# A second bank for the products with v of the later query blocks, and a later weight-norm sum, in a hybrid attention and mLSTM block

## The chip, the core and the metric

The kernel is one program on one core of a Trainium2 chip. The metric is device time in microseconds of a whole execution: 1434.75 us before the change, the median of three runs (1434.04, 1434.75 and 1437.02).

## What is computed

One layer of a streaming encoder block over a sequence of 1024 positions and 1024 channels. Inputs are normalised and multiplied with one wide projection; its columns feed a differential-attention branch with 8 heads and an mLSTM branch with 8 heads. Both are gated, projected, merged, projected once more and added to the input, and a last norm follows. The change touches the attention branch and the preparation of weights. For one head and one block of 128 queries the reference computes

```
logits = einsum("pbhqd,pbhkd->pbhqk", qb, k) + bias          # p: the two halves of the head
probs  = softmax(where(mask, logits, NEG_INF), axis=-1)
attn   = probs[0] - lam * probs[1]
out    = einsum("bhqk,bhkv->bhqv", attn, v)
```

and then normalises `out` over its 128 columns, scales it and multiplies it by SiLU of a gate.

## The kernel before

All large products are done in float16 with the operands split into a high and a low half, so that one product takes three matmuls (high by high, high by low, low by high). TensorE streams one long list of such projections, in "units" of 256 weight columns. A unit is either plain (96 matmuls of 512 columns, lines 329 to 331) or by rows (192 matmuls of 256 columns, lines 358 to 360). A unit takes 32 steps of the main loop. Beside the unit that runs, the loop issues in each step a piece of the next unit's preparation and pieces of one "side": the attention of a head or the mLSTM of a head. An attention head h runs beside the two units (q and k, then v and gate) of head h+1, that is 288 matmuls, 64 steps. The last head, 7, runs beside four gate units.

**Preparation of a unit** (`prep`). ScalarE squares and sums the two halves of the weights (line 245), VectorE adds the two sums (line 159), a matmul with ones adds them over the partitions (line 165), VectorE makes a power of two out of it (lines 135 to 139), and then ScalarE and VectorE write the high and the low half of the weights in four pieces each (lines 257 and 259). Between the squares and the sum there are two empty steps.

**Attention of a head** (`attention`). There are eight query blocks i = 0 to 7; block i has (i+1) x 128 keys. Its pieces are:
- `q` i: the first scores (line 812, into the two-bank tile psb), VectorE adds the bias and takes the extremum (line 822), ScalarE takes the exponential (line 826).
- `r` i: the second scores in the same way, then the combination of the two (line 837), and its split into a high and a low half (ScalarE line 844, VectorE line 845), which one DMA transposes (line 847, in SyncE's queue).
- `v` i: the product with v, 3 x (i+1) matmuls of 128 columns (lines 855 to 857) into a quarter of a bank, and ScalarE's sum of squares of it (line 858). Four blocks share one bank.
- `f` half: GpSimd makes the norm factors of four blocks (lines 862 to 864). `o` half: VectorE scales the four quarters of the bank by them and by the gate (line 870). `t` half: the result is split and transposed (lines 547 to 549).

**What sets the order.** `PLAN_A` gives for each piece the step of the unit loop at which it is issued (the number times 8/7), for heads 0 to 6; `PLAN_C` does it for head 7, and is not changed. A scheduler then orders the issued instructions of each engine anew: an instruction issued earlier has the higher claim, but one whose operands or whose tile are not free by its own reckoning is passed by others. On the chip each engine then works through its list in order, and waits where a semaphore is not yet set.

**PSUM.** There are eight banks: three for the projections (pp), two as one tile for scores (psb), two for small products (pmi: transposes, norm sums, and in the mLSTM the state updates) and one for the products with v (pvp). Since pvp is one bank, block 4 of a head can begin only when VectorE has scaled blocks 0 to 3 out of it (line 870). Matmuls also wait for ScalarE's read of the bank they write: block 5 waits for the squares of block 4.

Of the kernel before, what the change touches and what calls it, by code (L numbers as in the profile page):

```python
# [32 lines left out]
OFF_GATE = (9232, 10256)  # L33
BIG = 3.0e38
RING = 15
PLAN_A = [(0, 'q0'), (0, 'r0'), (0, 'q1'), (3, 'r1'), (4, 'q2'), (5, 'r2'), (9, 'q3'), (9, 'r3'), (9, 'q4'), (10, 'v0'), (14, 'v1'), (16, 'r4'), (17, 'q5'), (18, 'v2'), (19, 'r5'), (21, 'q6'), (24, 'r6'), (25, 'q7'), (27, 'r7'), (28, 'v3'), (29, 'v4'), (29, 'v5'), (30, 'f0'), (30, 'o0'), (31, 'v6'), (31, 'v7'), (42, 't0'), (55, 'f1'), (55, 'o1'), (55, 't1')]
PLAN_C = [(0, 'q0'), (0, 'r0'), (6, 'q1'), (7, 'r1'), (7, 'q2'), (9, 'r2'), (16, 'q3'), (19, 'r3'), (19, 'q4'), (19, 'r4'), (19, 'v0'), (22, 'v1'), (22, 'v2'), (25, 'q5'), (28, 'r5'), (29, 'q6'), (31, 'v3'), (32, 'v4'), (33, 'r6'), (37, 'q7'), (38, 'f0'), (38, 'r7'), (46, 'o0'), (52, 'v5'), (52, 'v6'), (63, 'v7'), (64, 'f1'), (67, 'o1'), (82, 't1'), (83, 't0')]
PLAN_M = [(0, '00gate'), (0, '01k0'), (2, '02k1'), (4, '03s0'), (5, '04s1'), (8, '05e0'), (9, '06p0'), (11, '07e1'), (13, '08p1'), (14, '09c0'), (19, '10g00'), (19, '11g01'), (20, '12g02'), (21, '13cp0'), (22, '14bs0'), (22, '15g10'), (25, '16g11'), (25, '17g12'), (26, '18cp1'), (30, '19bs1'), (30, '20g20'), (30, '21g21'), (31, '22cp2'), (32, '23bs2'), (33, '24ch'), (37, '25n0'), (47, '26t0'), (50, '27n1'), (55, '28t1')]
PLAN_N = [(0, '00gate'), (1, '01k0'), (1, '02k1'), (8, '03s0'), (10, '04s1'), (13, '05e0'), (13, '06p0'), (15, '07e1'), (16, '08p1'), (22, '09c0'), (25, '10g00'), (26, '11g01'), (26, '12g02'), (26, '13cp0'), (30, '14bs0'), (31, '15g10'), (36, '16g11'), (37, '17g12'), (40, '18cp1'), (42, '19bs1'), (43, '20g20'), (44, '21g21'), (53, '22cp2'), (54, '23bs2'), (59, '24ch'), (61, '25n0'), (67, '26t0'), (70, '27n1'), (71, '28t1')]
# [9 lines left out]
def block_kernel(ctx, tc, x, norm_w, w_in, lam, subln_w, rel_bias, conv_w, conv_b, b_if,  # L49
# [18 lines left out]
    def nm(p):  # L68
        uid[0] += 1
        return f"{p}{uid[0]}"  # L70
# [5 lines left out]
    def R(dt=F32, shape=None, p="r"):  # L76
        return ring.tile(shape or [P, S], dt, tag="t4", name=nm(p))
# [7 lines left out]
    def sm(cols=1, dt=F32, p="s", bufs=6):  # L85
        return small.tile([P, cols], dt, tag=f"{p}{cols}", name=nm(p), bufs=bufs)
# [7 lines left out]
    def m_ps():  # L94
        return pmi.tile([P, 512], F32, tag="pmi", name=nm("pmi"))

    def v_ps():
        return pvp.tile([P, 512], F32, tag="pvp", name=nm("pvp"))

    def junk(w):  # L100
        return wpool.tile([P, S], BF, tag="junk", name=nm("junk"), bufs=1)[:, :w]
# [129 lines left out]
    def wparts(shape):  # L231
        return wpool.tile([P, 2] + shape, F16, tag="wp", name=nm("wp"), bufs=WP)

    def prep(w, rowscale=None, keep=False):
        wd = w.width
        if rowscale is not None:
            g.tensor_tensor(w.wt[0], w.wt[0], rowscale[:, 0:4].unsqueeze(2).to_broadcast([P, 4, wd]), op=ALU.mult)
            yield
            for k in range(4, 8):
                s.activation(w.wt[k // 4][:, k % 4, :], w.wt[k // 4][:, k % 4, :], AF.Copy, scale=rowscale[:, k:k + 1])  # L240
            yield
        ss = sm(cols=2, p="wss")
        for k in range(2):
            j = junk(4 * wd).rearrange("p (a b) -> p a b", a=4)
            s.activation(j, w.wt[k], AF.Square, accum_out=ss[:, k:k + 1])  # L245
            yield
        yield
        yield
        w.sb = sm(p="sb")
        w.isb = sm(p="isb", bufs=8)  # L250
        fnorm_finish(ss, w.sb, w.isb)
        yield
        w.parts = {}

        def split(name, src, dst):
            w.parts[name] = dst
            s.activation(dst[0], src, AF.Copy, scale=w.sb)  # L257
            yield
            v.scalar_tensor_tensor(dst[1], src, w.sb, dst[0], op0=ALU.mult, op1=ALU.subtract)  # L259
            yield  # L260

        if keep:
            t = [R(F16, [P, KC, 256], p="wo") for _ in range(2)]
        for k in range(0, KC, 2):
            src = w.wt[k // 4][:, k % 4:k % 4 + 2, :]
            if keep:
                dst = (t[0][:, k:k + 2, :], t[1][:, k:k + 2, :])
            else:
                u = wparts([2, 256])
                dst = (u[:, 0, :, :wd], u[:, 1, :, :wd])  # L270
            yield from split(k // 2, src, dst)
# [25 lines left out]
    class Unit:  # L297
# [13 lines left out]
        def start_prep(self):  # L311
            if self.prepping is None:
                self.finish_load()
                self.prepping = prep(self.w, self.rowscale and self.rowscale(), self.keep)
                self.left = 16

        def prep_step(self):
# [479 lines left out]
    def attention(h, plan):  # L797
        (Q, K, negc, strip), (vr, gz, eps) = live.pop(("qk", h)), live.pop(("vz", h))
        bb = BB
        v.tensor_copy(bb[:, 768:1024], strip)  # L800
        rr = sm(cols=16, p="rr", bufs=2)
        rc = sm(cols=16, p="rc", bufs=2)
        ssq = sm(cols=8, p="ssq", bufs=2)
        E, AT, ops, zs = {}, {}, {}, {}

        def qk(i, p):
            n = (i + 1) * P
            sp = s_ps()
            for c in range(0, n, 512):
                e = min(n, c + 512)  # L810
                for j in range(2):
                    te.matmul(sp[:, c:e], Q[:, p, i * P:(i + 1) * P], K[p][:, j, c:e],  # L812
                              start=(j == 0), stop=(j == 1))
            if i >= 4 or p == 0:
                z = R(p="z")
            else:
                z = zs.pop(i)
            if i < 4 and p == 0:
                zs[i] = z[:, 512:]
                z = z[:, :512]  # L820
            mx = sm(p="mx")
            v.tensor_tensor_reduce(z[:, :n], sp[:, :n], bb[:, S - n:], negc, BIG, op0=ALU.add,  # L822
                                   op1=ALU.min, accum_out=mx)
            if p == 0:
                v.tensor_scalar(mx, mx, lnc, None, op0=ALU.add)  # L825
            s.activation(z[:, :n], z[:, :n], AF.Exp, bias=mx, scale=-1.0,  # L826
                         accum_out=rr[:, 2 * i + p:2 * i + p + 1])
            E[i, p] = z

        def combine(i):  # L830
            n = (i + 1) * P
            v.reciprocal(rc[:, 2 * i:2 * i + 2], rr[:, 2 * i:2 * i + 2])
            nb = sm(p="nbeta")
            v.scalar_tensor_tensor(nb, rr[:, 2 * i:2 * i + 1], nlam, rc[:, 2 * i + 1:2 * i + 2],
                                   op0=ALU.mult, op1=ALU.mult)
            A = E[i, 0]
            v.scalar_tensor_tensor(A[:, :n], E[i, 1][:, :n], nb, A[:, :n], op0=ALU.mult, op1=ALU.add)

        def turn(i):

            n = (i + 1) * P
            A = E.pop((i, 0))
            hl = E.pop((i, 1)).bitcast(F16)
            s.activation(hl[:, :n], A[:, :n], AF.Copy)
            v.tensor_tensor(hl[:, n:2 * n], A[:, :n], hl[:, :n], op=ALU.subtract)
            AT[i] = b3(A.bitcast(F16))
            nc.sync.dma_start(AT[i][:, :2 * (i + 1), :], hl[:, :2 * n], transpose=True)

        def pv(i):
            if i % 4 == 0:  # L850
                ops[i // 4] = v_ps()
            o = ops[i // 4][:, i % 4 * P:(i % 4 + 1) * P]
            at = AT.pop(i)
            for j in range(i + 1):
                te.matmul(o, at[:, j, :], vr[:, 0, j, :], start=(j == 0), stop=False)  # L855
                te.matmul(o, at[:, j, :], vr[:, 1, j, :], start=False, stop=False)
                te.matmul(o, at[:, i + 1 + j, :], vr[:, 0, j, :], start=False, stop=(j == i))
            s.activation(junk(P), o, AF.Square, scale=rc[:, 2 * i:2 * i + 1], accum_out=ssq[:, i:i + 1])

        def factor_of(qh):  # L860
            f = fac[qh] = sm(cols=4, p="fac", bufs=2)
            g.tensor_scalar(f, ssq[:, qh * 4:qh * 4 + 4], 1.0 / P, eps, op0=ALU.mult, op1=ALU.add)
            g.tensor_tensor(f, f, mhalf[:, 0:4], op=ALU.pow)
            g.tensor_tensor(f, f, rc.rearrange("p (i two) -> p i two", two=2)[:, qh * 4:qh * 4 + 4, 0], op=ALU.mult)

        def scaled_of(qh):
            on[qh] = half_tile("on")
            for j in range(4):
                i = qh * 4 + j
                v.scalar_tensor_tensor(on[qh][:, j * P:(j + 1) * P], ops[qh][:, j * P:(j + 1) * P],  # L870
                                       fac[qh][:, j:j + 1], gz[:, i], op0=ALU.mult, op1=ALU.mult)

        def rows_of(qh):
            finish_y(h, qh, on[qh], -17)

        def both(i):
            qk(i, 1)
            combine(i)
            turn(i)

        fac, on = {}, {}
        pieces = dict(q=lambda i: qk(i, 0), r=both, v=pv, f=factor_of, o=scaled_of, t=rows_of)
        for _, name in plan:
            pieces[name[0]](int(name[1:]))
            yield
# [140 lines left out]
    for h in range(H - 1):  # L1026
        phases.append((da_units(h + 1), lambda h=h: attention(h, PLAN_A), PLAN_A))
    phases.append((ga, lambda: attention(H - 1, PLAN_C), PLAN_C))
# [7 lines left out]
    first = order[0]  # L1036
# [107 lines left out]
    for ch in range(4):  # L1144
        w, so = wo[ch].w, [None, None]
# [76 lines left out]
```

## Time and profile before

| | before |
|---|---|
| runs | 1434.04, 1434.75, 1437.02 us; median 1434.75 |
| profiled execution | 1435.78 us, of which the span of the instructions is 1433.9 us |
| granted TensorE clock, mean | 0.995 |
| VectorE, ScalarE, GpSimd busy | 848.0 us (59%), 735.0 us (51%), 157.5 us (11%) |
| stage of heads 0 to 7, about | 90 to 580 us |

The profile is of one execution. Matmuls are pipelined: one of 256 columns is shown as 0.27 us long, but they follow each other at 0.11 us. An "idle" time of TensorE in the rows is therefore what remains when the one before has been shown to its end, and is some 0.16 us less than what was lost. In the timeline rows the columns are: start in us from the span's start, duration, engine, line, operation, output and inputs, form, count, and in brackets the idle time before it with what ended it.

### The profile page before, as it was taken

The numbers are of one execution on the slowest core, as the hardware profiler recorded it, in microseconds if no ns is written. First come the engines' busy times: TensorE is split into PE (matmuls) and PEld (weight loads), VectorE is DVE, ScalarE is ACT, GpSimd is POOL, SyncE is SP. The second block draws the span as 40 slices with busy tenths as digits, with TensorE's granted clock in tenths as the row PEclk, the third lists the DMA queues.
The fourth block names the chain that finished last, engine by engine and source line by source line (L and its number), as shares of the span: only waits on it lengthen the run. The fifth ranks groups of instructions, "written<-read, shape, count | busy, mean of one in ns | idle before, by whom it ended". The sixth has DMA issues, their size and how long they took to land.

```text
span 1433.9 us, 25050 instructions
## 1 busy us (share of the span) xinstructions
PE 1380.6 (96%) x9650; PEld 913.3 (64%) x9650; DVE 848.0 (59%) x2310; ACT 735.0 (51%) x1533; POOL 157.5 (11%) x215
## 2 busy tenths in 40 slices
PE   6989999999999999999999999999999999999997
PEld 3656575665756655444486787778769675444786
DVE  6276868677686756533445674775866564233633
ACT  7276556565566667832353444443435344644542
POOL 2001010010100100100102020220211200122004
PEclk9999999999999999999999999999999999999999
DMA  6456355463554645543321313231232135534303
GB/s 200 68 142 140 83 107 124 104 141 82 114 121 91 136 95 130 163 149 125 96 74 60 104 31 101 47 87 47 66 97 75 60 86 158 168 103 162 118 16 118
DMA packets 232585, 150.14 MB, mean 105 GB/s; under 512 B 117297, under 2 KB 209730, under 8 KB 232466
## 3 DMA queue, kind: packets, MB, share of 16 engines
q1 hardware_dynamic: 218450, 123.28, 35.0%
q10 hardware_dynamic: 14016, 25.27, 5.3%
q8 instruction: 75, 1.23, 0.3%
q14 instruction: 44, 0.36, 0.1%
HBM read 90.12 MB, written 18.55 MB: 76 GB/s over the span
## 4 chain that ended last, share of the span: by engine, by line
PE 77%; DVE 9%; ACT 4%; DMA 4%; POOL 3%; issue 3%; SPq 0%; POOLq 0%; DVEq 0%; ACTq 0%
PE pp L329 14%; PE pp L331 14%; PE pp L330 14%; PE pp L360 8%; PE pp L358 8%; PE pp L359 8%; PE psb L812 3%; DVE z L822 3%; DMA z<-z 2%; ACT z L826 1%; DMA qw<-rows_d 1%; DVE wp L259 1%; PE psb L908 1%; PE pvp L855 1%; DVE hl L600 1%
## 5 line engine op out<-in xcount | busy, mean ns | idle before, releaser
L358 PE MATMUL pp<-wp,X 128*128 128x256 f16 x1280 | 349.7, 273 | 0.0
L359 PE MATMUL pp<-wp,X 128*128 128x256 f16 x1280 | 349.7, 273 | 0.0
L360 PE MATMUL pp<-wp,X 128*128 128x256 f16 x1280 | 349.7, 273 | 0.0
L329 PE MATMUL pp<-X,wp 128*128 128x512 f16 x768 | 291.7, 380 | 0.3 <-ACT wp L257 0.3
L331 PE MATMUL pp<-X,wp 128*128 128x512 f16 x768 | 291.3, 379 | 0.6 <-DVE wp L259 0.6
L330 PE MATMUL pp<-X,wp 128*128 128x512 f16 x768 | 291.8, 380 | 0.0
L257 ACT ACTIVATE wp<-wt,sb 128x512 f16<-128x512 f32 x208 | 136.9, 711 | 105.4 <-DVE sb L138 70.6
L331 PEld LDWEIGHTS <-wp 128*128 128x128 f16 x1024 | 100.0, 98 | 119.7 <-DVE wp L259 1.2
L245 ACT ACTIVATE junk<-wt 128x1024 bf16<-128x1024 f32 x112 | 118.1, 1055 | 100.0 <-DMA wt<-in_w_in_dram 89.7
L329 PEld LDWEIGHTS <-wp 128*128 128x128 f16 x1024 | 100.2, 98 | 103.0 <-issue 1.7
L330 PEld LDWEIGHTS <-wp 128*128 128x128 f16 x1024 | 100.1, 98 | 97.1
L259 DVE SCALAR_TENSOR_TENSOR wp<-wt,sb,wp 128x512 f16<-128x512 f32 x208 | 150.5, 760 | 14.4 <-ACT wp L257 12.8
L359 PEld LDWEIGHTS <-X 128*128 128x128 f16 x1280 | 125.3, 98 | 18.4 <-issue 2.4
L358 PEld LDWEIGHTS <-X 128*128 128x128 f16 x1280 | 125.4, 98 | 16.8 <-issue 0.8
L360 PEld LDWEIGHTS <-X 128*128 128x128 f16 x1280 | 125.3, 98 | 14.6
L826 ACT ACTIVATE z<-z,mx 128x256 f32<-128x256 f32 (+7 forms) x128 | 99.0, 773 | 61.7 <-DVE mx L825 46.1
L822 DVE CUSTOM_DVE_ANT_0 z<-psb,BB,negc 128x256 f32<-128x256 f32 (+7 forms) x128 | 104.1, 813 | 19.7 <-PE psb L812 19.4
L331 PE MATMUL pp<-Y,wp 128*128 128x512 f16 x256 | 97.1, 379 | 0.0
L330 PE MATMUL pp<-Y,wp 128*128 128x512 f16 x256 | 97.1, 379 | 0.0
L329 PE MATMUL pp<-Y,wp 128*128 128x512 f16 x256 | 97.1, 379 | 0.0
L649 DVE SCALAR_TENSOR_TENSOR acc<-up,wcol,acc 128x512 f32<-128x512 f32 x96 | 78.0, 827 | 27.4 <-POOL acc L650 24.5
L812 PE MATMUL psb<-K,Q 128*128 128x512 f16 (+3 forms) x384 | 83.5, 326 | 7.8 <-DMA K<-hl 4.6
(245 smaller groups left out, 2012.1 us busy)
## 6 DMA issues: line engine op xcount, KB each, us to landing
wt<-in_w_in_dram SPq DMA_DIRECT2D x128, 256.0 KB, 3.4
wt<-in_w_in_dram SPq DMA_DIRECT2D x24, 512.0 KB, 3.9
K<-hl SPq DMA_DIRECT2D x32, 256.0 KB, 3.7
gate_d<-tg ACTq DMA_DIRECT2D x32, 256.0 KB, 2.2
xt<-in_x_dram SPq DMA_DIRECT2D x8, 512.0 KB, 5.2
Q<-hl SPq DMA_DIRECT2D x32, 128.0 KB, 2.4
wt<-in_w_pa_dram SPq DMA_DIRECT2D x8, 512.0 KB, 5.4
ft<-gate_d ACTq DMA_DIRECT2D x16, 256.0 KB, 2.8
```

What stands on the lines that cost most here:

```text
L245: s.activation(j, w.wt[k], AF.Square, accum_out=ss[:, k:k + 1])
L257: s.activation(dst[0], src, AF.Copy, scale=w.sb)
L259: v.scalar_tensor_tensor(dst[1], src, w.sb, dst[0], op0=ALU.mult, op1=ALU.subtract)
L329: te.matmul(ps, wh, xh, start=(start and i == 0), stop=False, **kw)
L330: te.matmul(ps, wh, xl, start=False, stop=False, **kw)
L331: te.matmul(ps, wl, xh, start=False, stop=(stop and i == n - 1), **kw)
L358: te.matmul(ps[:, o], xh[:, t], wh, start=i == 0, stop=False)
L359: te.matmul(ps[:, o], xh[:, t], wl, start=False, stop=False)
L360: te.matmul(ps[:, o], xl[:, t], wh, start=False, stop=i == KC - 1)
L812: te.matmul(sp[:, c:e], Q[:, p, i * P:(i + 1) * P], K[p][:, j, c:e], start=(j == 0), stop=(j == 1))
L822: v.tensor_tensor_reduce(z[:, :n], sp[:, :n], bb[:, S - n:], negc, BIG, op0=ALU.add, op1=ALU.min, accum_out=mx)
L826: s.activation(z[:, :n], z[:, :n], AF.Exp, bias=mx, scale=-1.0, accum_out=rr[:, 2 * i + p:2 * i + p + 1])
```

## The change

Three edits:
1. `pv` takes the bank for blocks 4 to 7 from the small products (pmi) and not from pvp. Blocks 0 to 3 stay in pvp. This holds for both plans.
2. In `PLAN_A`, v6 and v7 move from 31 to 33 and 35, f1 from 55 to 43 and o1 from 55 to 44; t1 stays at 55.
3. `prep` has five empty steps between squares and sum in place of two; the very first unit keeps two.

```diff
-PLAN_A = [..., (31, 'v6'), (31, 'v7'), (42, 't0'), (55, 'f1'), (55, 'o1'), (55, 't1')]
+PLAN_A = [..., (33, 'v6'), (35, 'v7'), (42, 't0'), (43, 'f1'), (44, 'o1'), (55, 't1')]
...
-    def prep(w, rowscale=None, keep=False):
+    def prep(w, rowscale=None, keep=False, slack=5):
...
-        yield
-        yield
+        for _ in range(slack):
+            yield
         w.sb = sm(p="sb")
...
-                self.prepping = prep(self.w, self.rowscale and self.rowscale(), self.keep)
+                self.prepping = prep(self.w, self.rowscale and self.rowscale(), self.keep, 2 if self is first else 5)
...
         def pv(i):
             if i % 4 == 0:
-                ops[i // 4] = v_ps()
+                ops[i // 4] = m_ps() if i else v_ps()
```

The numbers of instructions of each kind are the same. Their order changes in all attention heads. Three places of head 1 follow; heads 0 to 5 read alike. Numbers behind a name's underscore only tell one buffer from another.

TensorE, from the end of block 3's product to block 4's. Before (between the two rows stand 37 matmuls of the projection, lines 358 to 360):

```order
L857 MATMUL pvp_1855<-vr_1290,z_1822 128x128
L358 LDWEIGHTS X_256
L358 MATMUL pp_2070<-wp_1813,X_256 128x256
...
L358 MATMUL pp_2070<-wp_1853,X_306 128x256
L855 LDWEIGHTS z_1845
L855 MATMUL pvp_2097<-vr_1290,z_1845 128x128
```

and now (six projection matmuls between):

```order
L857 MATMUL pvp_1850<-vr_1290,z_1818 128x128
L358 LDWEIGHTS X_256
L358 MATMUL pp_2070<-wp_1859,X_256 128x256
...
L360 MATMUL pp_2070<-wp_1859,X_256 128x256
L855 LDWEIGHTS z_1841
L855 MATMUL pmi_2097<-vr_1290,z_1841 128x128
```

Block 4 moved 31 projection matmuls ahead and into the other bank. Counted in projection matmuls from the start of the list, the products of blocks 3 to 7 stood at 678, 715, 720, 725 and 749, with a norm sum (line 165) at 736; now they stand at 678, 684, 689, 708 and 744, with the norm sum at 732. The norm sum near the head's beginning moved from 597 to 606. The second scores of block 2, which stand at 596 in both, are used below as a mark. The scores of blocks 6 and 7 (first, second) stood at 651, 664, 670 and 678, and stand now at 651, 660, 666 and 673.

VectorE, from the second scores of block 7 to the last half of its split (mx and z are the score tiles, on the scaled output, hl the split of k). Before:

```order
L822 ISA z_2038,mx_2039<-psb_2033,BB_95,negc_899 128x1024
L822 ISA mx_2039 128x1
L845 TENSOR_TENSOR z_2003<-z_1984,z_2003 128x896
L870 SCALAR_TENSOR_TENSOR on_2151<-pvp_1855,fac_2147,tz_1289 128x128 x2
L832 RECIPROCAL rc_1695<-rr_1694 128x2
L870 SCALAR_TENSOR_TENSOR on_2151<-pvp_1855,fac_2147,tz_1289 128x128
L834 SCALAR_TENSOR_TENSOR nbeta_2043<-rr_1694,nlam_141,rc_1695 128x1
L870 SCALAR_TENSOR_TENSOR on_2151<-pvp_1855,fac_2147,tz_1289 128x128
L837 SCALAR_TENSOR_TENSOR z_2022<-z_2038,nbeta_2043,z_2022 128x1024
L548 SCALAR_TENSOR_TENSOR y_2328<-on_2151,y_2328 128x512
L800 COPY BB_95<-strip_1680 128x256
L845 TENSOR_TENSOR z_2038<-z_2022,z_2038 128x1024
```

and now:

```order
L822 ISA z_2038,mx_2039<-psb_2033,BB_95,negc_899 128x1024
L822 ISA mx_2039 128x1
L845 TENSOR_TENSOR z_2003<-z_1984,z_2003 128x896
L600 SCALAR_TENSOR_TENSOR hl_1874<-pp_1975,hl_1874 128x512
L832 RECIPROCAL rc_1695<-rr_1694 128x2
L870 SCALAR_TENSOR_TENSOR on_2151<-pvp_1850,fac_2147,tz_1289 128x128
L834 SCALAR_TENSOR_TENSOR nbeta_2043<-rr_1694,nlam_141,rc_1695 128x1
L870 SCALAR_TENSOR_TENSOR on_2151<-pvp_1850,fac_2147,tz_1289 128x128
L837 SCALAR_TENSOR_TENSOR z_2022<-z_2038,nbeta_2043,z_2022 128x1024
L870 SCALAR_TENSOR_TENSOR on_2151<-pvp_1850,fac_2147,tz_1289 128x128 x2
L800 COPY BB_95<-strip_1680 128x256
L845 TENSOR_TENSOR z_2038<-z_2022,z_2038 128x1024
```

Two of the four scalings went behind the combination (line 837), and line 600, which stood ahead of the second scores of block 7, now stands behind them. Head 6 had this order of VectorE before the change too. Earlier in the head, two of the four low halves of the weights (line 259) stood ahead of the first scores of block 3; now all four stand behind them.

ScalarE, from the second exponential of block 7. Before:

```order
L826 ACTIVATE z_2038,rr_1694<-z_2038,mx_2039 128x1024
L547 ACTIVATE y_2328<-on_2151 128x512
L858 ACTIVATE junk_2113,ssq_1696<-pvp_2097,rc_1695 128x128
L844 ACTIVATE z_2038<-z_2022 128x1024
L567 ACTIVATE vr_2064<-pp_2070 128x256
L858 ACTIVATE junk_2133,ssq_1696<-pvp_2097,rc_1695 128x128
L245 ACTIVATE junk_2145,wss_2144<-wt_1732 128x1024
```

and now:

```order
L826 ACTIVATE z_2038,rr_1694<-z_2038,mx_2039 128x1024
L858 ACTIVATE junk_2113,ssq_1696<-pmi_2097,rc_1695 128x128
L858 ACTIVATE junk_2133,ssq_1696<-pmi_2097,rc_1695 128x128
L245 ACTIVATE junk_2145,wss_2144<-wt_1732 128x1024
L844 ACTIVATE z_2038<-z_2022 128x1024
L245 ACTIVATE junk_2162,wss_2144<-wt_1898 128x1024
```

The squares of blocks 4 and 5 and the first squares of the next weights now stand ahead of the high half of block 7 (line 844).

More of the change, by code (lines that the diff above doesn't have):

```diff
@@ L35 @@
 RING = 15
-PLAN_A = [(0, 'q0'), (0, 'r0'), (0, 'q1'), (3, 'r1'), (4, 'q2'), (5, 'r2'), (9, 'q3'), (9, 'r3'), (9, 'q4'), (10, 'v0'), (14, 'v1'), (16, 'r4'), (17, 'q5'), (18, 'v2'), (19, 'r5'), (21, 'q6'), (24, 'r6'), (25, 'q7'), (27, 'r7'), (28, 'v3'), (29, 'v4'), (29, 'v5'), (30, 'f0'), (30, 'o0'), (31, 'v6'), (31, 'v7'), (42, 't0'), (55, 'f1'), (55, 'o1'), (55, 't1')]
+PLAN_A = [(0, 'q0'), (0, 'r0'), (0, 'q1'), (3, 'r1'), (4, 'q2'), (5, 'r2'), (9, 'q3'), (9, 'r3'), (9, 'q4'), (10, 'v0'), (14, 'v1'), (16, 'r4'), (17, 'q5'), (18, 'v2'), (19, 'r5'), (21, 'q6'), (24, 'r6'), (25, 'q7'), (27, 'r7'), (28, 'v3'), (29, 'v4'), (29, 'v5'), (30, 'f0'), (30, 'o0'), (33, 'v6'), (35, 'v7'), (42, 't0'), (43, 'f1'), (44, 'o1'), (55, 't1')]
 PLAN_C = [(0, 'q0'), (0, 'r0'), (6, 'q1'), (7, 'r1'), (7, 'q2'), (9, 'r2'), (16, 'q3'), (19, 'r3'), (19, 'q4'), (19, 'r4'), (19, 'v0'), (22, 'v1'), (22, 'v2'), (25, 'q5'), (28, 'r5'), (29, 'q6'), (31, 'v3'), (32, 'v4'), (33, 'r6'), (37, 'q7'), (38, 'f0'), (38, 'r7'), (46, 'o0'), (52, 'v5'), (52, 'v6'), (63, 'v7'), (64, 'f1'), (67, 'o1'), (82, 't1'), (83, 't0')]
```

## The prediction

> **What bounds the kernel now.** I read the page's busy times first, then busy times by stage, then what TensorE waits for.
>
> ```profile
> PE 1380.6 (96%) x9650; PEld 913.3 (64%) x9650; DVE 848.0 (59%) x2310; ACT 735.0 (51%) x1533; POOL 157.5 (11%) x215
> ```
>
> TensorE is busy for 96% of the span. By stage (start and end in us, length, busy time of each engine with its count, granted clock):
>
> ```profile
> 160.80:221.60 60.80, 57.53 (x447) 38.40 (x446) 44.74 (x128) 37.65 (x86) 4.61 (x8) 1.00 0.54 111
> 584.00:700.00 116.00, 116.00 (x560) 53.35 (x559) 40.74 (x86) 46.23 (x80) 6.29 (x3) 1.00 0.46 143
> 1060.00:1180.00 120.00, 119.82 (x911) 91.64 (x910) 76.08 (x217) 52.98 (x110) 15.30 (x17) 1.00 0.26 72
> ```
>
> The first row is one head, head 1: TensorE idles 3.27 us in 60.80. The other two are gate and mLSTM stages: 0.00 and 0.18 us. So only the attention heads have anything to give, and only TensorE's waits there count. What they are:
>
> ```profile
> PE pvp L855 <- DVE on L870: 12.0, 8, 1.6
> PE pvp L855 <- DMA z<-z: 4.2, 5, 1.1
> ```
>
> Eight waits for line 870, one per head, are the wait for the single bank; five are for the transpose of block 7. In head 1's timeline of TensorE:
>
> ```profile
> 152.54 0.48 PE L812 MATMUL psb<-K,Q 128*128 128x384 f16 x2
> ...
> 183.15 0.27 PE L360 MATMUL pp<-wp,X 128*128 128x256 f16 x1
> 183.26 0.27 PE L358 MATMUL pp<-wp,X 128*128 128x256 f16 x1
> 185.12 0.22 PE L855 MATMUL pvp<-vr,z 128*128 128x128 f16 x1 [1.59 <-DVE on L870]
> ...
> 191.27 0.16 PE L165 MATMUL pmi<-s,ones 128*128 128x1 bf16 x1 [0.24 <-DVE s L159]
> ...
> 193.86 0.23 PE L855 MATMUL pvp<-vr,z 128*128 128x128 f16 x1 [0.98 <-DMA z<-z]
> ```
>
> Projection matmuls follow at 0.11 us (183.15, 183.26). Block 4's product starts 1.59 us late for the bank, and block 7's still 0.98 us late for its transpose. **This second wait is what decides.** TensorE takes its list in order, so whatever is saved ahead of block 7 is lost again there unless the transposed block lands earlier too. The path to it runs outside TensorE (SyncE, VectorE, ScalarE of head 1):
>
> ```profile
> 188.90 2.97 SPq L847 DMA_TRANSPOSE z<-z  x1
> ```
> ```profile
> 176.73 1.28 DVE L822 CUSTOM_DVE_ANT_0 z<-psb,BB,negc 128x1024 f32<-128x1024 f32 x1 [1.11 <-PE psb L812]
> ...
> 183.75 0.61 DVE L870 SCALAR_TENSOR_TENSOR on<-pvp,fac,tz 128x128 f32<-128x128 f32 x2 [1.53 <-POOL fac L864]
> ...
> 184.98 1.28 DVE L837 SCALAR_TENSOR_TENSOR z<-z,nbeta,z 128x1024 f32<-128x1024 f32 x1
> ...
> 187.65 1.23 DVE L845 TENSOR_TENSOR z<-z,z 128x1024 f16<-128x1024 f32 x1 [0.58 <-ACT z L844]
> ```
> ```profile
> 181.30 1.14 ACT L826 ACTIVATE z<-z,mx 128x1024 f32<-128x1024 f32 x1
> ...
> 186.57 1.04 ACT L844 ACTIVATE z<-z 128x1024 f16<-128x1024 f32 x1
> ...
> 188.48 1.06 ACT L245 ACTIVATE junk<-wt 128x1024 bf16<-128x1024 f32 x1
> ```
>
> The reader is to see one chain: exponential 181.30, scalings (they wait for GpSimd's factors, 1.53 us) 183.75, combination 184.98, high half 186.57, low half 187.65, transpose issued 188.90, landed 193.86, which is 4.96 us after issue. From the mark at 152.54 (second scores of block 2) to the exponential are 28.76 us, from there to the issue 7.60.
>
> **The change part by part.** Sums are for the profiled execution, 1435.78 us with a span of 1433.9; the median of the runs is 1434.75, 1.0 lower.
>
> *The bank.* Block 4 no longer waits for line 870: 1.59 us of idle, gone. Its own transpose was issued long before, so nothing else holds it. What is late next on TensorE: with block 4 only five matmuls ahead of block 5, block 5 waits for ScalarE's squares of block 4, which stand behind the exponential of 181.30. I put it at 0.5 us, bounded by nothing and by that exponential's 1.14. So TensorE would reach block 7 at 193.86 - 0.98 - 1.59 - 0.24 + 0.5, and 0.55 earlier because block 7 stands five matmuls nearer: **191.0**. (The 0.24 is the norm sum, taken below.) Block 7 lands later than that if the chain gains less than 2.9 us.
>
> *The chain.* A stretch of the trace shows nearly the new order: head 6, where no later q and k unit is interleaved, already has the scores of blocks 4 to 7 at the matmul counts that all heads now get, line 600 behind the last scores, and two of the four scalings behind the combination.
>
> ```profile
> 455.84 0.48 PE L812 MATMUL psb<-K,Q 128*128 128x384 f16 x2
> ```
> ```profile
> 469.96 1.02 DVE L822 CUSTOM_DVE_ANT_0 z<-psb,BB,negc 128x768 f32<-128x768 f32 x1 [0.90 <-PE psb L812]
> ...
> 479.35 1.28 DVE L822 CUSTOM_DVE_ANT_0 z<-psb,BB,negc 128x1024 f32<-128x1024 f32 x1
> ...
> 486.60 1.28 DVE L837 SCALAR_TENSOR_TENSOR z<-z,nbeta,z 128x1024 f32<-128x1024 f32 x1
> ```
> ```profile
> 483.50 1.14 ACT L826 ACTIVATE z<-z,mx 128x1024 f32<-128x1024 f32 x1
> ```
> ```profile
> 490.31 1.61 SPq L847 DMA_TRANSPOSE z<-z  x1
> ```
>
> Mark to exponential: 483.50 - 455.84 = 27.66, 1.10 less than in head 1. Exponential to combination: 3.10 against 3.68. Exponential to issue: 6.81 against 7.60. In the whole 1.89 us shorter.
>
> *Two things keep heads 0 to 5 from all of it.* First the later norm sum. It puts two more low halves of weights (line 259) between the scores.
>
> ```profile
> L259 DVE SCALAR_TENSOR_TENSOR wp<-wt,sb,wp 128x512 f16<-128x512 f32 x208 | 150.5, 760 | 14.4 <-ACT wp L257 12.8
> ```
>
> They cost 150.5 / 208 = 0.72 us each, 1.45 for two. The cover is VectorE's wait of 0.90 us for scores in head 6 (row at 469.96), so about 0.55 shows; the bounds are nothing and 1.45. Second, ScalarE now does the squares of blocks 4 and 5 and one L245 (1.06) ahead of the high half. Counted from the exponential: 1.2 until it is done, 0.5 until block 5's matmuls start, 18 of them at 0.06 and 0.3 for their end, 0.5 for the squares, 1.06: 4.6 us. The combination gives its result at 3.10 + 1.28 = 4.4, so 0.2 us is lost; were ScalarE free it would be nothing, and if the squares waited for a later block 5, up to the 1.06 of the L245. The issue then comes 1.89 - 0.55 - 0.2 = 1.15 us earlier, and block 7 lands at 192.7, after TensorE's 191.0. TensorE waits there 1.7 us.
>
> *What is given back.* Block 7 now has five matmuls fewer ahead and five more behind: 0.55 us. A head gains 1.15 - 0.55 = **0.6 us**; six heads, 3.6.
>
> *Heads 6 and 7.*
>
> ```profile
> 495.37 0.22 PE L855 MATMUL pvp<-vr,z 128*128 128x128 f16 x1
> ...
> 547.53 0.22 PE L855 MATMUL pvp<-vr,z 128*128 128x128 f16 x1 [1.46 <-DVE on L870]
> ```
>
> In head 6 block 7 starts at 495.37 with no wait; its transpose was issued at 490.31 and, at 4.96, landed about 495.3. The chain there has the new order already, so it gains 0.2, between 0.6 and a loss of 0.75 from the two low halves. Head 7 keeps its plan, and block 4 moves 18 matmuls ahead into the free bank: 1.46 goes, and some 0.4 comes back where the scores behind it meet VectorE earlier. 1.1, bounded by 0 and 1.6.
>
> *The rest costs nothing I can name.* f1 and o1 stand at the same place of VectorE's list as before (behind the low halves of the weights), and t1 is not moved. The later norm sums of the mLSTM and gate stages lie beside a TensorE with 0.18 us of idle in 120; their weights are ready several steps ahead of use, and 3 steps of a plain unit are 9 matmuls, 2 us. If that cover were gone, a unit would start up to 2 us late. In the first unit nothing moves. SyncE now issues three of the four copies of K ahead of block 7's transpose and one behind; they are read only by the next head, 15 us on.
>
> Sum: 3.6 + 0.2 + 1.1 = 4.9 us. 1435.8 - 4.9 = **1430.9 us**.
>
> **Rivals.**
> *(A) TensorE sets the pace, not the transpose.* If the chain is as fast as head 6's and ScalarE is free, block 7 lands at 191.9 or sooner, and nearly all the idle goes: 1.59 + 0.24 + 0.98 less 0.5 is 2.3 us a head, 13.8 in six, with 1.3 for the last two 1420.7. For it: head 6 reaches block 7 without a wait. Against: there TensorE had lost time to the bank first. The Trainium skill ("Perfetto Trace Analysis", Optimization Strategy) says that the same gap repeating on the engine that should be saturated can mean too few PSUM buffers; read so, the bank is all that was missing, and the time would be this rival's.
> *(B) The wait only moves.* The two low halves show in full (1.45): the chain gains 0.25, the five matmuls take 0.55, and the heads lose 0.3 each; with head 7's 1.1, 1436.5. With 0.9 shown it is 1433. Nothing to measure.
> *(C) Slower: the scores on VectorE.* Not two but all four low halves (2.9) lie open, because ScalarE's high halves, now dealt out between exponentials, come late and VectorE waits for each in its order. The chain is then 1.89 - 2.9 - 0.2 = 1.2 later, with the 0.55 a head loses 1.75: 10.5 in six, less 1.1: 1445.2. It turns to a loss once more than 1.15 us of them shows in a head. Against it: VectorE idled 1.11 us at 176.73 and 0.90 at 469.96.
> *(D) One long wait slows the clock.* At the start two waits of TensorE close together are followed by half speed:
>
> ```profile
> 76.86 0.37 PE L812 MATMUL psb<-K,Q 128*128 128x128 f16 x2 [2.47 <-DMA K<-hl]
> 79.34 0.37 PE L812 MATMUL psb<-K,Q 128*128 128x128 f16 x2 [2.10 <-DMA K<-hl]
> ```
> ```profile
> 79.40:82.40 3.00, 3.00 (x16) 2.14 (x17) 2.93 (x11) 2.72 (x9) 0.00 (x0) 0.50 1.10 305
> ```
>
> Over 3.0 us the clock was 0.50, which loses 1.5 us. If the waits gathered at block 7 did that in six heads, 9 us: 1440. The 1.59 us of head 1 did not (clock 1.00), and I expect 1.7. The Trainium skill ("TensorE: Matmul & The Clock Gate", What's actually happening) puts the drop after an idle window of about 3.4 us, free-running; the start's rows agree with it, and by it my 1.7 would not suffice.
> *(E) The bank is not free.* The norm sums use pmi too, and could wait for block 4 to 7's bank. But it has two banks, and between block 4 and o1 one norm sum is issued at a time. 1436; I give it no share of its own.
>
> **How the numbers follow.** Forecast 0.47, A 0.17, B 0.21, C 0.11, D 0.04. A difference of 0.2%, 2.9 us, is about what can be told from no change: faster is below 1431.9, slower above 1437.6. The forecast's own range is 1427 to 1434 (each head 0 to 1.3); two thirds of it count as faster with all of A, 0.5; B and a third of the forecast are the same, 0.36; C and D slower, 0.14. The range reaches from A at 1420 to B's far side, 1437, and leaves out C, D and A's tail.
>
> **What would show it.** Right: no wait for line 870 on the products with v; in heads 0 to 5 a wait of 1 to 2 us for the transpose at block 7, its issue about 35.2 us after the mark (36.36 now); line 844 right behind L245. A: no wait at block 7. B and C: the first scores of block 7 on VectorE later than 24.2 us after the mark, as now (176.73). D: clock below 1.00 in a head. Most likely to be wrong is the share of the low halves that shows.

## The result, and the profile after

| | before | after |
|---|---|---|
| median (range), us | 1434.84 (1434.04 to 1437.02), 4 runs | 1448.48 (1446.70 to 1452.10), 4 runs |
| ratio, 95% interval | | 1.0094 (1.0081 to 1.0106) |
| profiled execution, its span | 1435.78, 1433.9 | 1452.10, 1450.3 |

The change makes the kernel slower by 0.9%, 13.6 us by the medians; the two profiled executions differ by 16.3. Both lists of TensorE hold the same 7680 projection matmuls, so the starts of equal ones can be set side by side: the 2600th (the heads are done) starts at 589.8 us before and 583.1 after, 6.8 earlier. The 6500th (the mLSTM is done) starts at 1249.8 and 1266.4, 16.6 later. To the last one 0.2 is won back. So **the heads gained 6.8 us, and the mLSTM stages lost 23.4**. The profiled execution is the slowest of the four, 3.6 us above their median; in which stage the others lost less is not recorded. The page and the stretches say the same (columns as before):

```profile
PE 1386.2 (96%) x9650; PEld 916.6 (63%) x9650; DVE 848.0 (58%) x2310; ACT 735.9 (51%) x1533; POOL 158.9 (11%) x215
```
```profile
160.00:220.00 60.00, 57.21 (x451) 38.50 (x448) 45.00 (x128) 37.62 (x87) 4.62 (x8) 1.00 0.58 113
...
1060.00:1180.00 120.00, 114.27 (x864) 87.47 (x864) 73.73 (x216) 51.67 (x105) 14.88 (x17) 0.99 0.26 71
```

In 120 us of the mLSTM TensorE now idles 5.73, where it idled 0.18. TensorE's waits from 760 to 1250 us, first before, then after:

```profile
PE psb L947 <- DVE C L930: 0.9, 2, 0.7
```
```profile
PE psb L945 <- ACT num L951: 8.2, 5, 2.0
PE psb L947 <- DVE C L930: 5.6, 7, 0.9
PE psb L947 <- issue: 2.8, 2, 2.2
PE pmi L927 <- DVE nb L135: 0.4, 2, 0.2
```

Lines 945 and 947 are the mLSTM's products into the score banks (with v, and with the running state). They wait for ScalarE to copy earlier results out (line 951) and for VectorE to update the state (line 930). The waits grew by 16.1 us in all.

**What ScalarE was doing.** One of these places, in both kernels. ScalarE before, and the waiting product:

```profile
1012.40 1.06 ACT L245 ACTIVATE junk<-wt 128x1024 bf16<-128x1024 f32 x1 [1.26 <-DMA wt<-in_w_in_dram]
1015.02 1.06 ACT L245 ACTIVATE junk<-wt 128x1024 bf16<-128x1024 f32 x1 [1.47 <-DMA wt<-in_w_in_dram]
1016.08 0.47 ACT L951 ACTIVATE num<-psb 128x387 f32<-128x387 f32 x1
```
```profile
1017.52 0.27 PE L945 MATMUL psb<-vr,E 128*128 128x129 f32 x1
```

After:

```profile
1016.70 1.06 ACT L245 ACTIVATE junk<-wt 128x1024 bf16<-128x1024 f32 x1 [3.01 <-DMA wt<-in_w_in_dram]
1019.82 1.06 ACT L245 ACTIVATE junk<-wt 128x1024 bf16<-128x1024 f32 x1 [1.98 <-DMA wt<-in_w_in_dram]
1020.88 0.47 ACT L951 ACTIVATE num<-psb 128x387 f32<-128x387 f32 x1
```
```profile
1021.40 0.38 PE L945 MATMUL psb<-vr,E 128*128 128x129 f32 x1 [1.55 <-ACT num L951]
```

The order is the same. ScalarE stands at the squares of the next weights (line 245) because they have not landed, and the copy that TensorE needs stands behind them. Without its wait the product would have come at 1021.40 - 1.55 = 1019.85. The weights come late because the buffers come free late, each after the last low half (line 259) that reads the old weights in it. VectorE and SyncE's loads, before and then after:

```profile
1006.29 2.73 DVE L259 SCALAR_TENSOR_TENSOR wp<-wt,sb,wp 128x512 f16<-128x512 f32 x4
```
```profile
1007.73 1.81 SPq L226 DMA_DIRECT2D wt<-in_w_in_dram  x3
```
```profile
1011.40 2.08 DVE L259 SCALAR_TENSOR_TENSOR wp<-wt,sb,wp 128x512 f16<-128x512 f32 x3
1013.40 0.28 DVE L933 COPY C<-pmi 128x129 f32<-128x129 f32 x1
1013.72 0.75 DVE L259 SCALAR_TENSOR_TENSOR wp<-wt,sb,wp 128x512 f16<-128x512 f32 x1
```
```profile
1012.85 2.02 SPq L226 DMA_DIRECT2D wt<-in_w_in_dram  x3
```

The loads are issued 1017.52 - 1007.73 = 9.8 us ahead of the product before, and 1019.85 - 1012.85 = 7.0 us after. Three steps cost the loads 2.8 us of lead. Before, the copy ended at 1016.08 + 0.47 = 1016.55, 0.97 us ahead of the product; that was all the slack there was at this place.

At another place ScalarE's late copy is that of a projection (line 345, at 1073.09, behind squares that waited 3.21). GpSimd's and VectorE's convolution (lines 650, 649) and two steps on the running state (lines 933, 930) come late behind it, and TensorE waits 2.21 and 0.91. The 2.21 is a part of what the list above puts down to "issue"; what ends right ahead of the matmul, which starts at 1075.62, is VectorE's copy of the state:

```profile
1075.23 0.28 DVE L933 COPY C<-pmi 128x129 f32<-128x129 f32 x1
```

**The heads** went roughly as forecast. TensorE's mark, ScalarE's second exponential of block 7, SyncE's transposes and TensorE's block 7, in head 1:

```profile
150.90 0.49 PE L812 MATMUL psb<-K,Q 128*128 128x384 f16 x2
```
```profile
178.29 1.14 ACT L826 ACTIVATE z<-z,mx 128x1024 f32<-128x1024 f32 x1
...
181.67 1.06 ACT L245 ACTIVATE junk<-wt 128x1024 bf16<-128x1024 f32 x1
182.72 1.04 ACT L844 ACTIVATE z<-z 128x1024 f16<-128x1024 f32 x1
```
```profile
185.05 3.95 SPq L847 DMA_TRANSPOSE z<-z  x1
```
```profile
190.75 0.23 PE L855 MATMUL pmi<-vr,z 128*128 128x128 f16 x1 [2.00 <-DMA z<-z]
```

Line 870 is waited for no more. Block 7 waits for its transpose in its place: 0.97, 2.00, 0.78, 1.81, 1.03 and 2.89 us in heads 0 to 5, and 1.09 in head 6 (the 1.03 is put down to ScalarE's line 257 by the profile).

### The profile page after: what moved, and what is told of

It reads as the page before. It is cut to its first block, busy times and chain, and to the rows that moved or that the text cites. A ratio compares the mean times of both kernels' runs of the same rounds, so it can differ in the third digit from the quotient of the medians.

```text
span 1450.3 us, 25049 instructions
## 1 busy us (share of the span) xinstructions
PE 1386.2 (96%) x9650; PEld 916.6 (63%) x9650; DVE 848.0 (58%) x2310; ACT 735.9 (51%) x1533; POOL 158.9 (11%) x215
## 4 chain that ended last, share of the span: by engine, by line
PE 70%; DVE 10%; ACT 6%; DMA 5%; issue 5%; POOL 3%; SPq 0%; POOLq 0%; DVEq 0%; ACTq 0%
PE pp L329 12%; PE pp L331 12%; PE pp L330 12%; PE pp L358 8%; PE pp L359 8%; PE pp L360 8%; PE psb L812 3%; DMA z<-z 2%; DVE acc L649 2%; DVE z L822 2%; ACT z L826 1%; DMA qw<-rows_d 1%; POOL acc L650 1%; ACT wp L257 1%; ACT z L844 1%
## 5 line engine op out<-in xcount | busy, mean ns | idle before, releaser
L259 DVE SCALAR_TENSOR_TENSOR wp<-wt,sb,wp 128x512 f16<-128x512 f32 x208 | 147.1, 751 | 16.5 <-ACT wp L257 15.0
L358 PEld LDWEIGHTS <-X 128*128 128x128 f16 x1280 | 125.8, 98 | 16.6 <-issue 0.7
L359 PEld LDWEIGHTS <-X 128*128 128x128 f16 x1280 | 125.7, 98 | 16.1
```

The source lines that it names most:

```text
L358: te.matmul(ps[:, o], xh[:, t], wh, start=i == 0, stop=False)
L359: te.matmul(ps[:, o], xh[:, t], wl, start=False, stop=False)
```

## The experiments

"Heads" is how much later the 2600th projection matmul starts than before, "mLSTM" what comes on top of that by the 6500th; both in us, from the profiled executions. Ratios are to the kernel before on the same chip.

| run | median us | ratio (95%) | heads | mLSTM |
|---|---|---|---|---|
| the change | 1448.48 | 1.0094 (1.0081 to 1.0106) | -6.8 | +23.4 |
| e1_att_slack | 1428.14 | 0.9943 (0.9931 to 0.9955) | -8.1 | +0.9 |
| e2_sq_late | 1447.85 | 1.0084 (1.0071 to 1.0097) | -7.2 | +18.5 |
| e3_wt4 | 1446.27 | 1.0073 (1.0059 to 1.0087) | -9.2 | +17.5 |
| e4_slack_only | 1446.74 | 1.0068 (1.0056 to 1.0080) | -6.4 | +19.9 |
| e8_sq_const | 1428.16 | 0.9944 (0.9931 to 0.9958) | -7.5 | -0.3 |
| e9_halves_late | 1429.27 | 0.9950 (0.9935 to 0.9965) | -6.4 | +0.8 |
| e7_att_slack_only | 1428.71 | 0.9947 (0.9935 to 0.9959) | -7.9 | -0.2 |
| e5_no_slack | 1430.58 | 0.9961 (0.9948 to 0.9973) | -5.5 | -0.3 |
| e11_v7_40 | 1418.08 | 0.9878 (0.9865 to 0.9892) | -17.2 | 0.0 |
| e14_v7_41 | 1417.03 | 0.9872 (0.9858 to 0.9885) | -19.2 | -0.2 |
| e13_v7_42 | 1415.64 | 0.9860 (0.9845 to 0.9875) | -19.1 | +0.1 |
| e12_slack1 | 1428.09 | 0.9949 (0.9936 to 0.9961) | -8.6 | -0.8 |

### Where the loss comes from

**The later norm sum in attention's units alone.**

```diff
-  ... self.keep, 2 if self is first else 5)
+  ... self.keep, 5 if self.kind in ("aqk", "avz") and self is not first else 2)
```

> The changed kernel, with the norm sum three steps later in attention's units (aqk, avz) alone; the gate, projection and mLSTM units keep two steps. In the profile of the change the heads gained 6.8 us and the stages from 780 to 1245 us lost 23.4. Theory W (the later norm sums hold the weight buffers longer, the next weights come late, and ScalarE stands at their squares) and rival N (the norm sums and low halves themselves stand at bad places beside the mLSTM's recurrence) both expect the loss gone and the gain kept: 1428 us, 1426 to 1430. Rival O (the loss has another origin in the change, not the three steps of the mLSTM units) expects 1445 to 1449.

1428.14: the loss is gone, the gain kept. O falls; W and N agree here.

**The squares three steps later as well, outside attention** (three empty steps ahead of the squares, two behind).

> The changed kernel, with the squares of the weights (line 245) three steps later too in every unit that is not attention's; norm sums and low halves stay where the change put them, so the weight buffers come free as late as in the change. W: the weights have landed when ScalarE reaches the squares, its waits for them in the mLSTM stages fall from 64 us to under 50, and the copies behind them are on time: 1428 to 1432 us. N: nothing changes for the norm sums, 1446 to 1450.

1447.85, as N has it. But the squares did not move: the scheduler put them at the same place of ScalarE's list, ahead of the copy (line 951 is 953 here):

```profile
1018.87 1.06 ACT L247 ACTIVATE junk<-wt 128x1024 bf16<-128x1024 f32 x1 [1.95 <-DMA wt<-in_w_in_dram]
1019.92 0.47 ACT L953 ACTIVATE num<-psb 128x387 f32<-128x387 f32 x1
```

So this run didn't test W.

**Four weight buffers.**

```diff
-WT = 3
+WT = 4
```

> The changed kernel with four buffers for half weights instead of three; the order of all computation stays. W: the second half of a unit's weights no longer waits for the low halves of the unit before, so the loss of 23 us goes: 1425 to 1430 us, with no wait of TensorE for lines 930 and 951. N: the norm sums stand where they stood, 1445 to 1449.

1446.27, in the range of N and missed by W. A fourth buffer holds one more half, not a unit; the scheduler used it to put the next half's squares ahead of the copy, and these waited in turn:

```profile
1014.97 1.06 ACT L245 ACTIVATE junk<-wt 128x1024 bf16<-128x1024 f32 x1 [2.91 <-DMA wt<-in_w_in_dram]
1018.99 1.06 ACT L245 ACTIVATE junk<-wt 128x1024 bf16<-128x1024 f32 x1 [2.87 <-DMA wt<-in_w_in_dram]
1020.04 0.47 ACT L951 ACTIVATE num<-psb 128x387 f32<-128x387 f32 x1
```

In the change and in both these runs ScalarE stands at squares whose load is late; neither run took that wait away. The next one does.

**Squares of a constant tile in the mLSTM and last gate units.**

```diff
+    still = ctile([P, 4, 256], p="still")
+    g.memset(still, 0.03)
...
-            s.activation(j, w.wt[k], AF.Square, ...)
+            s.activation(j, w.wt[k] if w.real else still[:, :, :wd], AF.Square, ...)
```

> The changed kernel; in the mLSTM and last gate units ScalarE squares a constant tile instead of the weights (the weights' scale is left out of the computation there), so ScalarE no longer waits for a load at the squares. All else, the late norm sums and the late low halves too, stays. W (the loads come late, ScalarE stands at the squares, and the copies behind them hold up TensorE): most of the 23 us goes, 1426 to 1434 us, and TensorE's wait for line 951 goes with it. N (norm sums and low halves stand at bad places beside the recurrence): 1444 to 1450, since these have not moved.

1428.16, as W has it. Here are the loads, the low halves, ScalarE and the same product (lines 226, 259, 951 and 945 are 227, 263, 955 and 949):

```profile
1003.28 2.02 SPq L227 DMA_DIRECT2D wt<-in_w_in_dram  x3
```
```profile
1001.84 2.08 DVE L263 SCALAR_TENSOR_TENSOR wp<-wt,sb,wp 128x512 f16<-128x512 f32 x3 [1.12 <-ACT wp L261]
1004.16 0.75 DVE L263 SCALAR_TENSOR_TENSOR wp<-wt,sb,wp 128x512 f16<-128x512 f32 x1
```
```profile
1007.84 0.49 ACT L955 ACTIVATE num<-psb 128x387 f32<-128x387 f32 x1 [3.19 <-PE psb L951]
```
```profile
1009.80 0.39 PE L949 MATMUL psb<-vr,E 128*128 128x129 f32 x2
```

The loads lead the product by 1009.80 - 1003.28 = 6.5 us, no more than in the change (7.0), and nothing is lost: the copy now waits for TensorE, not TensorE for the copy. The norm sums stand at the same places of TensorE's list as in the change, so N falls with it. Not all else stayed: with no load to wait for, the scheduler put the squares far ahead (74 of them stand before the first copy of line 951, in the change 61), so the run takes the waiting squares out of the copies' way altogether. Late loads and late low halves do no harm here by themselves; they harm through ScalarE, which stands at the squares with the copies behind them.

**The norm sum at its old place, the halves held back** (outside attention: two empty steps ahead of the norm sum, three behind it).

> The changed kernel; outside attention the norm sum is back at two steps, but three empty steps now stand between it and the high and low halves of the weights. W: what counts is when the low halves let go of the weight buffer, and that is as late as in the change: 1442 to 1450 us. Rival N1 (the place of the norm sum itself, its matmul and its integer steps on VectorE, does the harm): 1427 to 1431.

1429.27, the number of N1, but the run does not decide between the two, because the halves were not held back. With the norm sum done, the scheduler put them where they stood before, and the loads are out in time (line 945 is 947 here):

```profile
1001.34 1.69 SPq L226 DMA_DIRECT2D wt<-in_w_in_dram  x3
```
```profile
1011.13 0.27 PE L947 MATMUL psb<-vr,E 128*128 128x129 f32 x1
```

1011.13 - 1001.34 = 9.8 us of lead, as before the change. The run shows that the norm sum is what sets the halves' place, not the step at which they are issued. What settles it for W is the run before it: the norm sum as late as in the change, and no loss.

**One empty step outside attention.**

```diff
-  ... 5 if self.kind in ("aqk", "avz") and self is not first else 2)
+  ... 5 if self.kind in ("aqk", "avz") and self is not first else 2 if self is first else 1)
```

> The change with the later norm sums in attention alone, and one empty step instead of two in all other units. W, turned round (an earlier norm sum lets go of the weight buffers earlier): the mLSTM stages of the kernel before have 2.8 us of stalls, so at most that is gained, 1425.5 to 1428.5. If the two steps were just enough and ScalarE's squares have not landed one step earlier, the norm sum stalls TensorE itself: 1430 to 1434.

1428.09, no different from two steps: two are early enough already, and the sum does not stall at one.

### Where the heads' gain comes from

**The later norm sums alone, in all units.**

> The kernel before with nothing but the norm sums three steps later in all units but the first. All theories that put the loss in these three steps (W, N) expect the mLSTM's 23 us in full, and of the heads' gain at most the part that the later norm sum brings (0 to 2 us): 1456 to 1459 us. O expects 1433 to 1437.

1446.74, 10 us below what W and N expected, and above O's range. The mLSTM lost 19.9, near the 23 expected; it was the heads that surprised, with 6.4 us from the norm sum alone.

**The same in attention's units alone.**

> The kernel before with the norm sums of attention's units three steps later and nothing else: neither the bank nor the plan. In the run with all units' norm sums later the heads gained 6.4 us with the bank still waited for (8.8 us in all). Theory S (in the heads the later norm sum alone lets the scheduler put the chain to block 7 in the order of head 6, and that is nearly the whole gain): 1428 to 1430.5 us. Rival B (bank and plan carry the gain, as the prediction has it): 1433 to 1436.

1428.71, as S has it: as much as the change with all three edits there (1428.14, the intervals lie on each other). TensorE's two largest waits in the heads (90 to 560 us):

```profile
PE pvp L855 <- DVE on L870: 8.8, 8, 1.5
PE pvp L855 <- ACT junk L858: 3.0, 7, 0.4
```

The bank is still waited for in every head (8.8 us, 12.0 before), but block 7's transpose is not the next on the list, and comes earlier. In head 1 it is issued 39.22 us after the head's first score product, against 41.37 before and 39.16 in the change. The later norm sum also brings the new order: counted in projection matmuls, the scores of block 6 (second) and block 7 stand at 660, 666 and 673 here, as in the change, where they stood at 664, 670 and 678 before.

**Bank and plan without the later norm sums.**

> The change without the later norm sums: two steps in all units; bank and plan as changed. S: the bank's wait only moves to block 7's transpose and what the plan adds is small: 1432 to 1436 us, no more than 3 us below the kernel before. The prediction (bank and chain, with two low halves fewer in the way, so 0.55 us a head better): 1427 to 1430.

1430.58: between the two, below S's range and 0.6 above the prediction's. So bank and plan do bring something by themselves, 5.5 us; with the norm sum, which brings 7.9 alone, they add nearly nothing (8.1 together). A part of that is the clock: with all three edits TensorE ran at half clock for 3.41 us in head 5, some 1.7 us lost (last section), and with the norm sum alone it did not. The order is the old one here, the three scores at 664, 670 and 678, and in head 1 the transpose of block 7 is issued 187.88 - 150.94 = 36.94 us after the mark, no earlier than before (36.36). What holds TensorE now is the norm sum, which the prediction had at 0.24 a head:

```profile
PE pmi L165 <- DVE s L159: 8.8, 7, 1.6
...
PE pmi L855 <- DMA z<-z: 3.8, 11, 0.9
```

**Block 7 later in the plan.** With the later norm sums in attention alone, what is left in the heads is the wait for block 7's transpose. These three fill it with projections:

```diff
-  (33, 'v6'), (35, 'v7'), (42, 't0'), (43, 'f1'), (44, 'o1'), (55, 't1')
+  (33, 'v6'), (42, 'v7'), (42, 't0'), (50, 'f1'), (51, 'o1'), (55, 't1')
```

(40, 48, 49 and 41, 49, 50 in the other two.)

> The change with the later norm sums in attention alone, and besides the pieces v7, f1, o1 at 40, 48, 49 of the plan: block 7's matmuls stand 12 projection matmuls (1.3 us) later. Theory F (block 7's wait for its transpose, 0.8 to 2.7 us in each of seven heads, 9.5 us in all, is open time that projections can fill): 2.1 us of it stay, 1421 us, 1420 to 1424. Rival M (projections taken ahead are missing behind block 7, so the wait moves to the end of the head): 1427 to 1429.

> As the run with v7 at 40, with v7, f1, o1 at 41, 49, 50: block 7 stands 18 projection matmuls (2.0 us) later than in the change. F: 0.7 us of the waits stay, 1419.5 us, 1418.5 to 1423. M: 1427 to 1430.

> As the run with v7 at 40, with v7, f1, o1 at 42, 50, 51: block 7 stands 30 projection matmuls (3.3 us) later than in the change. F: no wait for the transpose is left, 1418.5 us, 1417.5 to 1423. M: 1427 to 1430.

1418.08, 1417.03 and 1415.64: F holds against M, but each is 2 to 3 us better than its number, and below its range. In the heads of the last, the wait for the transpose is nearly gone:

```profile
PE psb L812 <- DVE mx L822: 3.8, 9, 1.9
...
PE pmi L855 <- DMA z<-z: 0.2, 1, 0.2
```

At **1415.64 us** (ratio 0.986) this version beats both kernels. A part of what exceeds F's number is head 5. With the later norm sums in attention alone and block 7 at its place in the change (1428.14) the long wait there halved the clock from 426.48 to 429.89 us, some 1.7 us lost. The traces of these three runs have no such stretch from 100 to 1395 us. What the rest is I did not find.

## Why the prediction was wrong

- **"The rest costs nothing I can name"** is the step that failed, with 23.4 us where it put none. It asked whether the later norm sum would make the mLSTM's projections wait for their weights, and found them "ready several steps ahead of use". They were: no projection waits for its weights in the list of waits. Its 9 matmuls, 2 us, for three steps were not far off either (2.8 us at the loads). What it did not ask is what the low halves let go of: three buffers for half weights, on which the next load waits, on which ScalarE waits in its list, with TensorE's copies behind. The Trainium skill ("TensorE: Matmul & The Clock Gate", the table at its head) calls ScalarE's queue a strict FIFO; the rows at 1019.82 and 1020.88 agree, where a copy starts right as squares end that had waited 1.98 us. The rows of before would have warned: ScalarE waited 1.26 and 1.47 us for these loads there already, and the copy behind them ended 0.97 us ahead of the product that needs it, less than the 2.8 that the loads lost.
- Of the 23.4 us, 16.1 are listed waits. Two stretches of 3.41 us at half clock behind them (last section) lose some 2 x 1.7 = 3.4. If each of the 14 further waits also costs the 0.16 us that a row of an idle TensorE leaves out, as worked out for the projections, that is 2.2, an estimate. The last 1.7 I did not assign.
- **The bank** went as written: no wait for line 870, and TensorE ready for block 7 at 190.75 - 2.00 = 188.75, 37.85 us after the mark (forecast 191.0 - 152.54 = 38.46).
- **The chain** was mis-sized, and one cause of it had the wrong sign. The issue came 185.05 - 150.90 = 34.15 us after the mark, 2.21 earlier than before, where 1.15 was forecast. The exponential came at 27.39, earlier than in head 6 (27.66), so the two low halves, charged with 0.55, cost nothing. The later norm sum was booked as a cost; alone it shortened the chain as much as the whole change and brought the scores into the order of head 6, from which the sum had it only take away. Without it bank and plan gained 5.5 us, with the chain no shorter (36.94 us). The landing gave some back: 190.75 - 185.05 = 5.70 us for 4.96.
- **Wait only moves**: right in kind. 1 to 2 us at block 7 were forecast, 0.78 to 2.89 came, and line 844 stands right behind line 245. Heads 0 to 5 gained 5.5 us against 3.6 (in spite of some 1.7 lost at half clock in head 5), head 6 0.6 against 0.2. Head 7 gained 0.45 against 1.1, because its wait moved to the scores and cost 1.26 there:

```profile
544.29 0.59 PE L812 MATMUL psb<-K,Q 128*128 128x512 f16 x2 [1.26 <-DVE mx L822]
```

- **The rivals.** A falls, since block 7 waits in every head but the last; "the bank is all that was missing" does not hold here. B falls by the chain. C had the sign of the result, but its mechanism did not occur: the first scores of block 7 came on VectorE at 174.14 - 150.90 = 23.24 us, not later than 24.2. D occurred, in one head and twice in the mLSTM. The prediction reads the start's rows as agreeing with a drop after one long idle window; they do not. In the profile before, the clock was 1.00 from 75.00 to 75.75 us and 0.50 from 75.85, within the first wait (74.39 to 76.86), so after less than 1.5 us of it. E: no such wait is listed. None of the rivals looked at the mLSTM, and so the range ended at 1437.

## What to carry to other kernels

When an edit made for one stage sits in a helper that other stages use, price it there by what its instructions release (a buffer, a load, the queue behind the load), not only by when their results are needed. Before spending slack, look whether an in-order engine already waits for the transfer in question: then what is left is only the time between the end of what stands behind it and its use (0.97 us here). A wait that is removed from a long list in order turns up in part at the next late operand; the rest is won when that operand's consumer is moved behind work that is ready, as with block 7 here (19 us in the heads in place of 7).

## What the hardware showed beside this

Half clock after waits of TensorE, in the profile after. The waiting matmuls: 2.89 us in head 5, 1.96 and 1.92 in the mLSTM (and 2.00 in head 1, shown above).

```profile
428.38 0.23 PE L855 MATMUL pmi<-vr,z 128*128 128x128 f16 x1 [2.89 <-DMA z<-z]
```
```profile
1199.70 0.38 PE L945 MATMUL psb<-vr,E 128*128 128x129 f32 x1 [1.96 <-ACT num L951]
```
```profile
1149.27 0.38 PE L945 MATMUL psb<-vr,E 128*128 128x129 f32 x1 [1.92 <-ACT num L951]
```

From 100 to 1395 us, this trace's record of the clock has three stretches at 0.50, each 3.41 us long. They start at 428.66, 1077.19 and 1200.07 us, which are 190 and 36 times 3.413 us apart. So time can be cut into steps of that length, and a drop starts at the border of two. The rows show steps ahead of a drop, the two drops, and the steps that hold the waits at 1149 and 191 (the third value from the end is the granted clock; TensorE's idle time is the length less its busy time, the second and third value):

```profile
425.25:428.66 3.41, 0.52 (x8) 0.28 (x6) 3.38 (x11) 2.48 (x4) 1.08 (x2) 1.00 1.06 208
428.68:432.05 3.37, 3.37 (x29) 3.00 (x27) 0.20 (x1) 1.01 (x3) 0.40 (x2) 0.50 1.00 247
1196.66:1200.07 3.41, 1.46 (x9) 0.66 (x7) 0.39 (x2) 1.53 (x3) 0.00 (x0) 1.00 0.25 73
1200.09:1203.46 3.37, 3.37 (x12) 1.66 (x12) 0.90 (x6) 1.06 (x2) 0.00 (x0) 0.50 0.26 93
1145.46:1148.87 3.41, 1.90 (x9) 0.69 (x7) 0.77 (x3) 1.18 (x3) 0.00 (x0) 1.00 0.80 316
1148.87:1152.28 3.41, 3.01 (x18) 2.02 (x19) 2.12 (x8) 0.84 (x2) 2.47 (x3) 1.00 0.05 19
186.32:189.73 3.41, 2.43 (x24) 1.93 (x21) 2.54 (x14) 1.98 (x5) 0.55 (x2) 1.00 1.16 138
189.73:193.14 3.41, 2.39 (x34) 2.29 (x35) 2.40 (x4) 2.00 (x6) 0.75 (x2) 1.00 0.98 182
```

Ahead of the drops TensorE was idle for 3.41 - 0.52 = 2.89 and 3.41 - 1.46 = 1.95 us of a step. Ahead of the one at 1077 it was 2.50, from two waits (2.21 and 0.91). The waits at 1149 and 191 are about as long as the one at 1200, but a border cuts them into 1.51 and 0.40, and into 0.98 and 1.02, and the clock stayed at 1.00. In the traces of all runs here, from 100 to 1395 us, each step with over 2 us idle was followed by 3.41 us at half clock, and none with under 1.88; of four steps between 1.88 and 1.96, three were. A drop costs half of 3.41, some 1.7 us, so a wait of 2 us can cost nearly as much again. The Trainium skill ("TensorE: Matmul & The Clock Gate", What's actually happening) puts the drop after an idle window of about 3.4 us, free-running. The 3.41 us steps agree; that the whole window must be idle does not, since 1.95 us were enough.
